# dt from x/rms under a scaled w_dt, the third block of x loaded one step earlier, and a new order of the opening

## The chip, the cores and the metric

The kernel runs on one core of one Trainium2 chip. Its engines work side by side, each through its own queue in order: PE (TensorE, the matmuls; "PEld" in the profile is its loading of weights), DVE (VectorE), ACT (ScalarE), POOL (GpSimd) and SP (SyncE), which here only issues DMAs. The metric is the device time of one execution in microseconds; less is better.

## The reference

One step of a streaming encoder layer for a prompt of 1024 tokens and a sample of 32, width 1024:

```python
shift, scale, gate = split(silu(c) @ w_ada + b_ada, 3)
hn   = rmsnorm(x, norm_g) * (1 + scale) + shift
proj = hn @ w_in       # lru_x | lru_gate | xBC | z | dt_raw, 1024+1024+1536+1024+16 columns
...
dt = softplus(dt_raw + dt_bias)
# RG-LRU on lru_x, chunked SSD scan on xBC with dt, grouped RMSNorm, gates
out = x + gate * (concat[y_lru, y_ssd] @ w_out)
y = rmsnorm(out, final_norm_g)
```

`dt_raw` is the last 16 columns of the projection, one per SSD head. The convolution and scan states are further outputs.

## The kernel before

All activations lie with channels on the 128 partitions and tokens along the free axis. The 1056 tokens are cut into three blocks: 384, 384 and 256 + 32 (the last 32 are the sample, which has its own scale and shift). A projection of 128 output columns is called a unit; for each block it takes 8 channel groups times 3 matmuls, since every fp32 operand is split in a rounded part (`whi`, `hb[..., 0]`) and a rest (`wlo`, `hb[..., 1]`): hi x hi, hi x lo, lo x hi.

The **opening** is what comes before the main loops. It must make `hb` (x/rms times the scale, as hi and lo) for the three blocks out of x and of `w_ada`, and meanwhile it computes the first three units (24, 25, 26) with what is ready. Its order on all engines is written by hand as a list of tokens, `PROG` (lines 46 to 60), under a manual schedule; a loop (lines 373 to 457) turns each token into instructions, and each engine runs its own in that order. The tokens that matter here, with block b and channel group k:

- `q`, `a`, `f`: squares of x on ACT (L179), their sums on DVE (L182, L185). `c`, `r`, `v`, `b`: sum over channels on PE (L192), root, reciprocal, spread over partitions on PE (L211). `x`: x times 1/rms in place, two groups at a time, on DVE (L217).
- `s`, `o`, `k`, `A`: a pair of `w_ada` units on PE (L120, fp32, 32 weight columns, four partition quarters in turn), its row on ACT (L424), columns of it on PE (L127), the scale `Acol` on DVE (L428). Pairs 0, 2, 4, 6 are the scale's, 8, 10, 12, 14 the shift's, whose columns come at once in `K`; `S` makes the shift (L433) and puts it in two extra columns of the third block's `hb`.
- `h`, `l`: `hb` hi on ACT (L224) and lo on DVE (L228) for one group of one block. `H`, `L`: the split of a unit's weight (L405, L409). `m`, `t`: a group's two hi matmuls and its lo matmul for one unit (L355). `p`: a finished bank is parked in SBUF (L363). `z`: dummy matmuls.
- `w`, `W`: `w_dt` split in hi and lo (L438, L440) as 32 weight columns. `d`, `D`: dt of a block out of `hb` hi and lo (L284, 16 matmuls a block; the shift goes through the two extra columns). `e`, `E`: copies of dt to `dtp` (L289). At the end the shift's part is added (L459) and dt is turned to tokens on partitions and its two halves summed by `selD` (L467).

Loads stand in a second list, `LOADS` (line 45), issued by SP in that order: `x00` is block 0 from group 0, `w` a unit's weight, `s` a `w_ada` pair of 1 MB (three buffers: the next one waits until its buffer's pair was used), `d` is `w_dt`. x has two buffers, so block 2 (`x20`, `x24`) can be loaded only when block 0 has been read for the last time: by `l07`.

The work behind the opening is ordered by a scheduler that simulates the program: units 27 and 16, then for each of eight SSD head pairs two units and the pair's small matmuls (transposes xsT, states dS, yd, yo), then the RG-LRU groups and the output projection, whose ACT and DVE orders are partly by hand.

Of the kernel before, what the change touches and what calls it, by code (L numbers as in the profile page):

```python
# [8 lines left out]
F32 = mybir.dt.float32  # L9
F32R = mybir.dt.float32r  # L10
# [3 lines left out]
D = 1024  # L14
# [29 lines left out]
FIRST = (24, 25, 26)  # L44
LOADS = "x00 x02 x04 x06 w s w s w s x10 x14 s d s s s s x20 x24".split()
PROG = (
# [13 lines left out]
).split()  # L60
# [3 lines left out]
def encoder_step(ctx: ExitStack, tc: tile.TileContext, a, o):  # L64
# [203 lines left out]
    wdt = st.tile([128, KT, 16], F32, name="wdt")  # L268
    wd = st.tile([128, KT, 32], F32R, name="wd")
    dtp = st.tile([32, TW], F32, name="dtp")  # L270
    dsb = st.tile([32, 2], F32, name="dsb")
    selD = st.tile([32, 16], F32, name="selD")
    root = st.tile([128, 1], F32, name="root")
# [4 lines left out]

    def dt_half(b, i):
        if i == 0:  # L280
            pds[b] = pbank([32, BLK[b][1]], "pdt")
        for kk in range(4 * i, 4 * i + 4):
            for q in range(2):
                nc.tensor.matmul(pds[b], lhsT=wd[:, kk, :], rhs=hb[b][:, kk, q, :], start=(kk + q == 0),  # L284
                                 stop=(kk + q == KT))

# [19 lines left out]
    with tc.manual_schedule(engines={E.SP, E.PE, E.Activation, E.DVE, E.Pool}):  # L306
# [8 lines left out]
        for i in (64, 96):  # L315
            nc.gpsimd.tensor_add(sel, sel, ident[:, i:i + 32])
        nc.gpsimd.tensor_add(selD, ident[0:32, 0:16], ident[0:32, 16:32])

# [7 lines left out]
        left_loads = list(LOADS)  # L326
        seen = set()


        def load_next():  # L330
            t = left_loads[0]
            if t == "s":
                n = len(sraw)
                if n >= 3 and 2 * n - 6 not in paired:
                    return False
                sraw.append(st.tile([128, 2, KT, 128], F32, name="sraw", tag="sraw", bufs=3))
                u = (2 * n + KT) % (2 * KT)
                last[0] = dma(sraw[n], a["w_ada"][u:u + 2].rearrange("i p k n -> p i k n"))
            elif t == "w":
                ws.append(fetch_unit(a["w_in"][FIRST[len(ws)]]))  # L340
            elif t == "d":
                dma(wdt, a["w_dt"])
            else:
                if t == "x20" and "l07" not in seen:
                    return False
                last[0] = load_x(int(t[1]), int(t[2]))
            left_loads.pop(0)
            return True

        last, paired = [None], set()  # L350

# [21 lines left out]
        for t in PROG:  # L373
            while left_loads and load_next():
                pass
            c = t[0]
            n = [int(q) for q in t[1:]] if c in "qxhlmtdac" else int(t[1:] or 0)
            if c == "z":
# [58 lines left out]
            elif c == "w":  # L437
                nc.scalar.copy(wd[:, :, 0:16], wdt)  # L438
            elif c == "W":
                nc.vector.tensor_sub(wd[:, :, 16:32], wdt, wd[:, :, 0:16].bitcast(F32))  # L440
            elif c == "d":
                dt_half(*n)
            elif c == "e":
                dt_out(n)
            elif c == "D":
                dt_half(2, 0)
                dt_half(2, 1)
            elif c == "E":
                dt_out(2)
                nc.vector.tensor_copy(dsb, pds[2][:, 288:290])  # L450
            elif c == "y":
# [13 lines left out]
    for c in range(9):  # L465
        t0, L = (c * 128, 128) if c < 8 else (S0, TS)
        nc.tensor.matmul(pt[0:L, c, :], lhsT=dtp[:, t0:t0 + L], rhs=selD, start=True, stop=True)  # L467
    for (L, c0, n) in ((128, 0, 8), (32, 8, 1)):
# [644 lines left out]
```

## Time and profile before

| | us |
|---|---|
| runs: median (lowest to highest of 3) | 776.29 (775.0 to 776.35) |
| the profiled execution | 775.32 |
| its span in the profile | 773.6 |

The profile takes one execution; 1.7 us of its time lie outside the span. A row of the time line reads: start, length, engine, line of the kernel, operation, output<-inputs, and in brackets the engine's idle time before it with what ended that. A row of the table by stretches reads: the stretch, its length, then busy time and count of PE, PEld, DVE, ACT and POOL (or of PE alone), the clock granted to PE as a share of the full one, the busy share of the DMA engines, and GB/s.

### The profile page before, as it was taken

The page shows a single profiled execution, that of the slowest core. Times are in us where ns is not written, and L with a number is a line of the kernel's source. Part 1 is how long each engine was busy: PE and PEld are TensorE (multiplying, and loading weights), DVE is VectorE, ACT ScalarE, POOL GpSimd, SP SyncE. Part 2 cuts the span into 40 slices and gives each one's busy share as a digit, 9 for nine tenths or more (in the row PEclk, how much of TensorE's full clock was granted, in tenths as well). Part 3 has the DMA queues.
Part 4 walks back from the last instruction along what each step waited for, and adds up shares of the span by engine and source line. Part 5 has one row for each costly group of instructions (what it writes and reads, how often), then busy time and mean ns, then how long its engine had stood idle before and what let it go on. Part 6 is the DMA issues. An engine that isn't in the chain of part 4 may idle for free.

```text
span 773.6 us, 12733 instructions
## 1 busy us (share of the span) xinstructions
PE 756.6 (98%) x5100; PEld 730.2 (94%) x5100; DVE 533.2 (69%) x861; ACT 413.3 (53%) x599; POOL 46.7 (6%) x159
## 2 busy tenths in 40 slices
PE   8989999999999999999999999999999999999994
PEld 8868999999999999999999999999999999999994
DVE  5754877888878777788376557546668897535643
ACT  5544764334426344253676977696777664323430
POOL 1000310001000000000011001100101000000000
PEclk9999999999999999999999999999999999999998
DMA  9750124443343434333222112011144685654841
GB/s 331 305 198 28 58 59 122 133 161 112 123 134 100 149 111 122 111 99 124 80 62 65 61 35 62 28 54 42 44 140 136 192 281 164 221 147 137 261 118 69
DMA packets 40059, 96.31 MB, mean 124 GB/s; under 512 B 4408, under 2 KB 22080, under 8 KB 40000
## 3 DMA queue, kind: packets, MB, share of 16 engines
q1 hardware_dynamic: 40000, 95.49, 38.8%
q8 instruction: 40, 0.66, 0.3%
q14 instruction: 19, 0.16, 0.1%
HBM read 85.53 MB, written 9.95 MB: 123 GB/s over the span
## 4 chain that ended last, share of the span: by engine, by line
PE 85%; DVE 6%; DMA 5%; ACT 2%; issue 1%; SPq 1%; POOL 0%; POOLq 0%; DVEq 0%; ACTq 0%
PE pj L236 16%; PE pj L238 16%; PE pj L237 16%; PE mix L943 6%; PE mix L941 6%; PE mix L942 6%; PE pj L355 3%; PE yd L688 2%; PE dS L663 2%; DMA sraw<-in_w_ada_dram 2%; PE yo L703 2%; PE ada_s L120 1%; PE xsT L647 1%; PE gt L825 1%; PE gt L827 1%; PE gt L826 1%
## 5 line engine op out<-in xcount | busy, mean ns | idle before, releaser
L236 PE MATMUL pj<-hb,whi 128*128 128x384 f32 (+1 forms) x792 | 260.1, 328 | 0.0
L237 PE MATMUL pj<-hb,whi 128*128 128x384 f32 (+1 forms) x792 | 259.5, 328 | 0.0
L238 PE MATMUL pj<-hb,wlo 128*128 128x384 f32 (+1 forms) x792 | 259.4, 327 | 0.0
L101 ACT CAST whi<-wraw 128x1024 fp32r<-128x1024 f32 x81 | 84.9, 1048 | 138.1 <-PE mix L942 68.4
L238 PEld LDWEIGHTS pj<-hb,wlo 128*128 128x128 f32 x792 | 150.0, 189 | 1.6 <-issue 1.5
L236 PEld LDWEIGHTS pj<-hb,whi 128*128 128x128 f32 x792 | 149.4, 189 | 1.9 <-issue 1.7
L237 PEld LDWEIGHTS pj<-hb,whi 128*128 128x128 f32 x792 | 150.0, 189 | 1.2 <-issue 1.1
L103 DVE TENSOR_TENSOR wlo<-wraw,whi 128x1024 fp32r<-128x1024 f32 x81 | 98.6, 1219 | 48.0 <-ACT whi L101 48.0
L943 PE MATMUL mix<-yt,wlo 128*128 128x324 f32 (+2 forms) x320 | 103.9, 326 | 0.4 <-DVE wlo L103 0.4
L941 PE MATMUL mix<-yt,whi 128*128 128x324 f32 (+2 forms) x320 | 104.1, 325 | 0.0
L942 PE MATMUL mix<-yt,whi 128*128 128x324 f32 (+2 forms) x320 | 103.7, 324 | 0.0
L498 DVE SCALAR_TENSOR_TENSOR u<-raw,par,u 128x1060 f32<-128x1060 f32 x60 | 78.5, 1311 | 1.5 <-ACT u L496 1.1
L943 PEld LDWEIGHTS mix<-yt,wlo 128*128 128x128 f32 x320 | 60.0, 188 | 0.8 <-DVE wlo L103 0.7
L941 PEld LDWEIGHTS mix<-yt,whi 128*128 128x128 f32 x320 | 60.1, 188 | 0.2
L942 PEld LDWEIGHTS mix<-yt,whi 128*128 128x128 f32 x320 | 60.0, 188 | 0.1
L255 ACT ACTIVATE raw<-pj,sb 128x256 f32<-128x256 f32 (+1 forms) x74 | 30.9, 468 | 25.4 <-PE pj L238 14.6
L631 DVE TENSOR_TENSOR_SCAN M<-M,mask 128x1060 f32<-128x1060 f32 x16 | 37.8, 2363 | 9.1 <-DMA M<-dA_d 9.1
L355 PE MATMUL pj<-hb,whi 128*128 128x384 f32 (+1 forms) x144 | 38.5, 339 | 2.5 <-ACT hb L224 2.5
L960 DVE SCALAR_TENSOR_TENSOR ot<-mix,gate,xr 128x352 f32<-128x352 f32 (+3 forms) x32 | 14.8, 489 | 26.2 <-PE mix L943 21.2
L355 PEld LDWEIGHTS pj<-hb,whi 128*128 128x128 f32 x144 | 25.1, 189 | 7.0 <-ACT hb L224 3.5
L634 ACT ACTIVATE M<-M 128x1060 f32<-128x1060 f32 x16 | 17.5, 1092 | 25.9 <-DVE M L631 24.0
L299 POOL COPY cso<-raw 128x3 f32<-128x3 f32 x20 | 15.8, 789 | 230.6 <-ACT raw L255 230.6
(231 smaller groups left out, 1098.7 us busy)
## 6 DMA issues: line engine op xcount, KB each, us to landing
wraw<-in_w_out_dram SPq DMA_DIRECT2D x48, 512.0 KB, 3.7
wraw<-in_w_in_dram SPq DMA_DIRECT2D x36, 512.0 KB, 3.7
M<-dA_d SPq DMA_DIRECT2D x16, 530.0 KB, 4.5
sraw<-in_w_ada_dram SPq DMA_DIRECT2D x8, 1024.0 KB, 11.2
E<-E_d SPq DMA_DIRECT2D x16, 265.0 KB, 4.4
yz_d<-y SPq DMA_DIRECT2D x8, 530.0 KB, 4.2
wraw<-in_w_ada_dram SPq DMA_DIRECT2D x8, 512.0 KB, 5.0
x<-in_xh_dram SPq DMA_DIRECT2D x4, 384.0 KB, 4.8
```

Source lines behind the costliest of these rows:

```text
L101: nc.scalar.copy(hi, raw)
L103: eng.tensor_sub(lo, raw, hi.bitcast(F32))
L236: nc.tensor.matmul(out, lhsT=hi[:, kk, :], rhs=hh, start=(kk == 0), stop=False)
L237: nc.tensor.matmul(out, lhsT=hi[:, kk, :], rhs=hl, start=False, stop=False)
L238: nc.tensor.matmul(out, lhsT=lo[:, kk, :], rhs=hh, start=False, stop=(kk == KT - 1))
L255: nc.scalar.activation(dst[0:P, off + d:off + d + e - s], banks[b][0:P, s:e], func, bias=sb[0:P, w:w + 1])
L355: nc.tensor.matmul(banks[u][b], lhsT=w[i][:, k, :], rhs=hb[b][:, k, 0 if heads else 1, :], start=(heads and k == 0 and i == 0), stop=(not ...
L498: nc.vector.scalar_tensor_tensor(u, raw[:, k:k + TW], wcol(k), u, op0=OP.mult, op1=OP.add)
L631: nc.vector.tensor_tensor_scan(M, M, mask, 0.0, op0=OP.add, op1=OP.mult)
L941: nc.tensor.matmul(ps, lhsT=w[0][:, k, :], rhs=yh, start=(half == 1 and k == 0), stop=False)
L942: nc.tensor.matmul(ps, lhsT=w[0][:, k, :], rhs=yl, start=False, stop=False)
L943: nc.tensor.matmul(ps, lhsT=w[1][:, k, :], rhs=yh, start=False, stop=(half == 0 and k == KT - 1))
```

## The change

It has three parts.

1. dt is no longer computed from `hb` but from x/rms itself: w_dt is multiplied by the scale (`wda`, one for the prompt, one for the sample), padded from 16 to 32 columns with zeros, and the eight channel groups go in fp32 into four partition quarters of one bank, two groups each. The shift's part is its own small product (`P`, `Q`) of `shift` with the unscaled, padded `wdp`. `dtp` has 128 rows now, and the transposing matmul sums the four quarters by `sel`. The copies of dt to `dtp` have 128 partitions instead of 32, the same columns.
2. In `LOADS` x's third block stands ahead of the last `w_ada` pair. It may be loaded when `l07` and `d0` are through, since `d0` now reads the first block's x.
3. `PROG` is a new order of all these tokens.

```diff
-LOADS = "x00 x02 x04 x06 w s w s w s x10 x14 s d s s s s x20 x24".split()
+LOADS = "x00 x02 x04 x06 w s w s w s x10 x14 s d s s s x20 x24 s".split()
 PROG = (
-        "z34 q00 q02 a02 q04 a04 q06 H0 a06 f0 L0 c0 s0 r0 v0 b0 o0 H1 k0 x00 A0 L1 h00 z6 s2 A1 l00 h01 m000 "
...
+    "z34 q00 q02 a02 q04 a04 q06 a06 H0 f0 L0 c0 r0 s0 v0 H1 b0 o0 L1 z1 k0 A0 A1 z1 s2 x00 x02 h00 o2 z1 "
...
-    wd = st.tile([128, KT, 32], F32R, name="wd")
-    dtp = st.tile([32, TW], F32, name="dtp")
-    dsb = st.tile([32, 2], F32, name="dsb")
-    selD = st.tile([32, 16], F32, name="selD")
+    wdp = st.tile([128, KT, 32], F32, name="wdp")
+    wda = st.tile([128, 2, KT, 32], F32, name="wda")
+    dtp = st.tile([128, TW], F32, name="dtp")
+    dsb = st.tile([128, 2], F32, name="dsb")
...
-    def dt_half(b, i):
-        if i == 0:
-            pds[b] = pbank([32, BLK[b][1]], "pdt")
-        for kk in range(4 * i, 4 * i + 4):
-            for q in range(2):
-                nc.tensor.matmul(pds[b], lhsT=wd[:, kk, :], rhs=hb[b][:, kk, q, :], start=(kk + q == 0),
-                                 stop=(kk + q == KT))
+    def dt_block(b):
+        pds[b] = pbank([128, XB[b][1]], "pdt")
+        for (s, e, w) in h_parts(b):
+            for kk in range(KT):
+                q = slice(32 * (kk % 4), 32 * (kk % 4) + 32)
+                nc.tensor.matmul(pds[b][q, s:e], lhsT=wda[:, w, kk, :], rhs=xin[b][:, kk, s:e], start=(kk < 4),
+                                 stop=(kk >= 4))
+
+    def dt_shift():
+        ps = pbank([128, 2], "pds")
+        for kk in range(KT):
+            q = slice(32 * (kk % 4), 32 * (kk % 4) + 32)
+            nc.tensor.matmul(ps[q, :], lhsT=wdp[:, kk, :], rhs=shift[:, kk, :], start=(kk < 4), stop=(kk >= 4))
+        return ps
...
-        nc.gpsimd.tensor_add(selD, ident[0:32, 0:16], ident[0:32, 16:32])
+        nc.gpsimd.memset(wdp, 0.0)
+        nc.gpsimd.memset(wda, 0.0)
...
-                if t == "x20" and "l07" not in seen:
+                if t == "x20" and not {"l07", "d0"} <= seen:
...
             elif c == "w":
-                nc.scalar.copy(wd[:, :, 0:16], wdt)
-            elif c == "W":
-                nc.vector.tensor_sub(wd[:, :, 16:32], wdt, wd[:, :, 0:16].bitcast(F32))
+                nc.gpsimd.tensor_copy(wdp[:, :, 0:16], wdt)
+                for w in range(2):
+                    nc.vector.tensor_mul(wda[:, w, :, 0:16], wdt, Acol[:, :, w:w + 1].to_broadcast([128, KT, 16]))
...
-        nc.tensor.matmul(pt[0:L, c, :], lhsT=dtp[:, t0:t0 + L], rhs=selD, start=True, stop=True)
+        nc.tensor.matmul(pt[0:L, c, :], lhsT=dtp[:, t0:t0 + L], rhs=sel[:, 0:16], start=True, stop=True)
```

What the new order does on ACT around the squares of x's third block (x_420). Before, with the second block's hb tiles as hb_84 and the third's as hb_85:

```order
L424 COPY hrow<-ada_s 128x256
L179 ACTIVATE xacc<-x_420 128x2x288
L179 ACTIVATE xsq<-x_420 128x2x288 x3
L224 ACTIVATE hb_84<-x_140,Acol 128x384 x4
L202 ACTIVATE xrs<-xbc,eps 128x2
L202 ACTIVATE xrs<-xbc,eps 32x1
L224 ACTIVATE hb_85<-x_420,Acol 128x256
```

The same place in the changed kernel:

```order
L224 ACTIVATE hb_84<-x_141,Acol 128x384 x3
L431 COPY hrow<-ada_s 128x256
L224 ACTIVATE hb_84<-x_141,Acol 128x384
L179 ACTIVATE xacc<-x_420 128x2x288
L179 ACTIVATE xsq<-x_420 128x2x288 x3
L224 ACTIVATE hb_84<-x_141,Acol 128x384
L431 COPY hrow<-ada_s 128x256
```

Four hb tiles of the second block stood behind the squares; one does now.

PE's dt matmuls stood together before: all of the shift's columns, then two blocks, and the third block's after its first unit:

```order
L355 MATMUL pj_461<-hb_84,whi 128x384
L127 MATMUL ada_c<-sel,hrow 128x2 x8
L284 MATMUL pdt<-hb_84,wd 32x384 x16
L284 MATMUL pdt<-hb_83,wd 32x384 x16
L355 MATMUL pj_669<-hb_85,whi 128x290
```

Now the first block's stands behind its last projection (first piece's place in the program), ahead of a `w_ada` pair:

```order
L211 MATMUL xbc<-ident,xrs 128x128 x3
L362 MATMUL pj_123<-hb_83,whi 128x384
L284 MATMUL pdt<-x_124,wda 32x384 x8
L120 MATMUL ada_s<-sraw,sc 32x256 x8
L362 MATMUL pj_445<-hb_84,whi 128x384
```

The first block's dt has moved from the end of the second block to the end of the first, with half as many matmuls, of fp32; the third block's stands within the second block's projections, and the second's at their end.

On DVE behind the opening, in the second head pair's loop: the convolution u of the next pair (three steps, L498) before, among the scans of M (L631) and the work on y:

```order
L498 SCALAR_TENSOR_TENSOR u<-raw,par,u 128x1060
L631 SCALAR_TENSOR_TENSOR M<-M,mask 128x1060
L707 TENSOR_TENSOR y<-y,yo 128x512
L248 COPY sb<-pj_1756 128x2
L635 TENSOR_TENSOR M<-M,CBm 128x1060
L707 TENSOR_TENSOR y<-y,yo 128x32
L498 SCALAR_TENSOR_TENSOR u<-raw,par,u 128x1060
L635 TENSOR_TENSOR M<-M,CBm 128x1060
L747 TENSOR_SCALAR gate<-ada_c,par 128x2
L498 SCALAR_TENSOR_TENSOR u<-raw,par,u 128x1060
```

and in the changed kernel (L503 is the same line, L636 the scan):

```order
L503 SCALAR_TENSOR_TENSOR u<-raw,par,u 128x1060
L677 SCALAR_TENSOR_TENSOR dS<-dS,dec_bc 128x64
L696 SCALAR_TENSOR_TENSOR y<-u,par,yd 128x512
L677 SCALAR_TENSOR_TENSOR dS<-dS,dec_bc 128x64
L503 SCALAR_TENSOR_TENSOR u<-raw,par,u 128x1060
L696 SCALAR_TENSOR_TENSOR y<-u,par,yd 128x32
L677 SCALAR_TENSOR_TENSOR dS<-dS,dec_bc 128x64 x2
L711 TENSOR_TENSOR yo<-yo,E 128x384
L248 COPY sb<-pj_1748 128x2
L503 SCALAR_TENSOR_TENSOR u<-raw,par,u 128x1060
L636 SCALAR_TENSOR_TENSOR M<-M,mask 128x1060
```

The convolution's three steps stand ahead of both scans now. On PE the transposes that read this u stand 49 projection matmuls earlier than before, at the 422nd behind the opening instead of the 471st.

More of the change, by code (lines that the diff above doesn't have):

```diff
@@ L326, in encoder_step @@
         left_loads = list(LOADS)
-        seen = set()
+        seen, last, paired = set(), [None], set()
         def load_next():
@@ L348, in load_next @@
             return True
-        last, paired = [None], set()
         def mm(u, b, k, heads):
@@ L376, in encoder_step @@
             c = t[0]
-            n = [int(q) for q in t[1:]] if c in "qxhlmtdac" else int(t[1:] or 0)
+            n = [int(q) for q in t[1:]] if c in "qxhlmtac" else int(t[1:] or 0)
             if c == "z":
@@ L437, in encoder_step @@
             elif c == "w":
-                nc.scalar.copy(wd[:, :, 0:16], wdt)
-            elif c == "W":
-                nc.vector.tensor_sub(wd[:, :, 16:32], wdt, wd[:, :, 0:16].bitcast(F32))
+                nc.gpsimd.tensor_copy(wdp[:, :, 0:16], wdt)
+                for w in range(2):
+                    nc.vector.tensor_mul(wda[:, w, :, 0:16], wdt, Acol[:, :, w:w + 1].to_broadcast([128, KT, 16]))
             elif c == "d":
-                dt_half(*n)
+                dt_block(n)
             elif c == "e":
                 dt_out(n)
[L445 to L450, printed above, removed]
+            elif c == "P":
+                aps["d"] = dt_shift()
+            elif c == "Q":
+                nc.vector.tensor_copy(dsb, aps["d"])
             elif c == "y":
```

24 rows, old and new, of the table PROG are left out of this document.

## The prediction

> **What bounds the kernel now.** I read the page first, then the chain that ended last, then the busy time of TensorE (PE) by stretches.
>
> ```profile
> PE 756.6 (98%) x5100; PEld 730.2 (94%) x5100; DVE 533.2 (69%) x861; ACT 413.3 (53%) x599; POOL 46.7 (6%) x159
> PE 85%; DVE 6%; DMA 5%; ACT 2%; issue 1%; SPq 1%; POOL 0%; POOLq 0%; DVEq 0%; ACTq 0%
> ...
> 38.00:52.00 14.00, 11.35 (x73) 9.61 (x72) 7.23 (x13) 7.00 (x15) 0.00 (x0) 1.00 0.75 273
> 200.00:400.00 200.00, 199.51 (x1452) 191.96 (x1451) 152.41 (x258) 90.58 (x121) 8.52 (x53) 1.00 0.36 113
> 400.00:600.00 200.00, 200.00 (x1237) 199.34 (x1236) 126.39 (x144) 154.07 (x214) 18.34 (x38) 1.00 0.23 68
> ```
>
> PE is the bound, and past the opening it hardly stops (199.51 of 200 us, then 200 of 200). So the time can fall in two ways only: PE gets less to do, or it waits less in the opening, the first 79.5 us, where the chain's DMA, DVE and ACT shares lie. Everything behind is then shifted as one piece, if its own chains on DVE and DMA come early too.
>
> Where does PE wait in the opening? In three places.
>
> ```profile
> 17.95 20.22 SPq L338 DMA_DIRECT2D sraw<-in_w_ada_dram  x4
> 38.26 0.97 SPq L171 DMA_DIRECT2D x<-in_xh_dram  x2
> ...
> 43.73 0.34 PE L355 MATMUL pj<-hb,whi 128*128 128x384 f32 x1
> 44.43 0.69 ACT L179 ACTIVATE xacc<-x 128x576 f32<-128x576 f32 x1 [3.83 <-DMA x<-in_xh_dram]
> 45.14 0.33 PE L355 MATMUL pj<-hb,wlo 128*128 128x384 f32 x1
> 45.93 1.27 ACT L179 ACTIVATE xsq<-x 128x576 f32<-128x576 f32 x2 [0.24 <-DMA x<-in_xh_dram]
> 47.10 2.12 ACT L224 ACTIVATE hb<-x,Acol 128x384 fp32r<-128x384 f32 x4
> 47.76 0.44 PE L355 MATMUL pj<-hb,whi 128*128 128x384 f32 x1 [2.28 <-ACT hb L224]
> ...
> 50.87 0.67 PEld L192 LDWEIGHTS xbc<-ones,xacc 128*128 128x128 f32 x6 [0.66 <-issue]
> ```
>
> ACT stands still for 3.83 us until the third block of x lands at 44.4, squares it, and only then makes the second block's hb tiles 4 to 7; PE wants tile 4 from 45.3 on and gets it at 47.76. The eight matmuls from 43.73 to 45.14 start 0.176 us apart, so the pause is 2.62 - 0.18 = **2.4 us**. The sum over the third block (L192) comes behind the same squares: 0.66 idle less a pitch, **0.5 us**.
>
> ```profile
> 69.01 0.19 PEld L355 LDWEIGHTS pj<-hb,whi 128*128 128x128 f32 x1 [0.49 <-ACT hb L224]
> 69.48 0.33 PEld L355 LDWEIGHTS pj<-hb,whi 128*128 128x128 f32 x2 [0.18 <-DVE hb L228]
> 70.09 0.33 PEld L355 LDWEIGHTS pj<-hb,whi 128*128 128x128 f32 x2 [0.17 <-DVE hb L228]
> 70.70 0.19 PEld L355 LDWEIGHTS pj<-hb,whi 128*128 128x128 f32 x1 [0.18 <-DVE hb L228]
> ```
>
> In the third block PE overtakes the hb tiles once more: 0.49 + 0.18 + 0.17 + 0.18 = **1.0 us**.
>
> **The change part by part.** *dt.* These rows carry it: the old dt matmuls, the shape nearest to the new ones, and a row of tiny ones.
>
> ```profile
> 59.26 1.84 PE L127 MATMUL ada_c<-sel,hrow 128*128 128x2 f32 x16
> 60.96 5.76 PE L284 MATMUL pdt<-hb,wd 128*32 128x384 f32 x32
> 70.94 2.29 PE L284 MATMUL pdt<-hb,wd 128*32 128x290 f32 x16
> 28.23 1.07 PE L120 MATMUL ada_s<-sraw,sc 128*32 128x256 f32 x16
> 28.91 0.28 DVE L440 TENSOR_TENSOR wd<-wdt,wd 128x128 fp32r<-128x128 f32 x1
> ```
>
> The old ones take PE from 60.96 to about 66.55 and from 70.94 to 73.07: 5.6 + 2.1 = 7.7 us with nothing beside them. The new ones have L120's pattern, plain fp32 with 32 weight columns, four partition quarters in turn (eight matmuls are sixteen records). L120 takes 1.07 us at 256 columns. At 384 columns I take 1.07 x 1.5, less its drain, 1.5 us, twice; 1.07 for the third block's 256 columns; and for its 32 columns and the shift's 2, where only L127's sixteen records in 1.84 us are near and have four times the weight columns, 0.45 each. Sum 5.0, so **-2.7 us**. Bounds: 3.2 us if columns cost nothing more and the small pieces nothing, 6.4 if the wide ones take 1.6 each and the small ones L120's 1.07: -4.5 to -1.3. Weights under the scale are two DVE products of L440's size (0.28 each) instead of one; they stand at about 33 us, between PE's first block's last tiles, for which DVE is some 0.8 us ahead. Were that cover gone, 0.3 us. ACT loses one cast. POOL (6% busy) clears two tiles and copies w_dt; behind that copy stand only the borders of the three parked tiles, which convolutions want some 40 us later.
>
> *The start.* The new order puts the second weight's rounding ahead of the first ada row on ACT.
>
> ```profile
> 14.01 0.37 ACT L424 COPY srow<-ada_s 128x256 f32<-128x256 f32 x1 [1.44 <-PE ada_s L120]
> 14.28 1.05 ACT L405 CAST whi<-wraw 128x1024 fp32r<-128x1024 f32 x1
> 15.86 1.22 DVE L409 TENSOR_TENSOR wlo<-wraw,whi 128x1024 fp32r<-128x1024 f32 x1
> 15.98 0.62 ACT L224 ACTIVATE hb<-x,Acol 128x384 fp32r<-128x384 f32 x1 [0.65 <-DVE Acol L428]
> 21.43 1.07 PE L120 MATMUL ada_s<-sraw,sc 128*32 128x256 f32 x16 [0.98 <-DMA sraw<-in_w_ada_dram]
> ```
>
> The cast starts with its weight's landing (about 14.05), ends at 15.1, the row copy at 15.5; on DVE the rest (1.22) now stands before Acol and x: 15.1 to 16.4, Acol to 16.75, x's first pair (0.95) to 17.7, and hb tile 0 comes at 18.4 instead of 16.6. PE's first projection starts at 18.45 instead of 17.62. But the third ada pair waits for its landing in both (21.43), and the fourth for its own (28.23). What remains is work not done by then: by the order 40 of the first block's 72 matmuls stand before the fourth pair, now 35. Five at 0.176: **+0.9 us**, paid later.
>
> *The third block of x.* Its DMA now waits for d0, which reads the first block's buffer, and stands ahead of the last ada pair. From 28.23 PE has: L120 and its switch 1.1, 37 matmuls 6.5, ada columns, sum and spread about 1.8, d0 1.5, so d0 ends near 39.1, 0.8 us after the old issue at 38.26. The transfer is then alone in the queue.
>
> ```profile
> wraw<-in_w_in_dram SPq DMA_DIRECT2D x36, 512.0 KB, 3.7
> x<-in_xh_dram SPq DMA_DIRECT2D x2, 576.0 KB, 6.2
> ```
>
> Against 6.2 us behind an ada pair I take 3.8 for it (the row of 512 KB): 43.0, its second half 44.5, the last pair near 47.1. On ACT hb tiles 0 to 6 of block two now stand before the squares, and tile 7 behind them is wanted only after 126 of the 144 matmuls of both blocks: the 2.4 us go. On PE the second block's first 42 matmuls (7.4) and three ada pairs (3.3) follow d0, so L192 comes at 49.8; DVE has its sum at about 48.9 (six tails and x's four products to 45.5, three additions 2.3, the last tail 0.6, the halves 0.45). That cover is 0.9 us: the 0.5 goes. Next: shift's columns end near 54.0, the shift itself 54.9, dt_shift at 55.7; x's last pair 56.0, where d2 starts at 56.2. Then 21 matmuls (3.7) and d1 give the third block a start near 62.9, with hb tiles ready by 61.1: the 1.0 goes.
>
> Sum: -2.7 - 2.4 - 0.5 - 1.0 + 0.9 = **-5.7 us** against the profiled execution's 775.32, so 769.6. The runs' median, 776.29, lies 0.97 above that execution; I forecast from the median: **770.6 us**.
>
> *Behind the opening* PE's order differs only by when small matmuls are slipped in, up to the fifth SSD head pair; I cost that at nothing, between -0.5 (what the row from 200 to 400 us loses) and the price of the first rival.
>
> **The rivals.**
>
> (a) The new order asks too early. By the order the third xsT stands 49 projection matmuls earlier.
>
> ```profile
> 173.48 1.32 DVE L498 SCALAR_TENSOR_TENSOR u<-raw,par,u 128x1060 f32<-128x1060 f32 x1
> 182.78 1.09 ACT L751 ACTIVATE u<-u 128x1060 f32<-128x1060 f32 x1 [0.73 <-DVE u L498]
> 185.53 1.15 PE L647 MATMUL xsT<-ident,u 128*128 128x128 f32 x9
> ```
>
> Its u was ready at 183.87, 1.7 us ahead. 49 x 0.162 (two wide pitches and one of 0.135) is 7.9 us; if DVE keeps its old pace PE waits 6.2 us and the result is 776.8, no change. Against it: DVE's order has moved the same convolution ahead of two scans of 2.4 us. For it: that planner's durations are not these rows. 12% for 3 us or more.
>
> (b) The third block lands as late as now, 6.2 us after its issue: 45.3, so L192 waits 2.4 - 0.9 = 1.5 us: 772.1. Its queue is empty then, which speaks against it. 10%.
>
> (c) The clock falls near the start.
>
> ```profile
> 46.25:49.66 3.41, 1.90 (x9) 1.00 0.82 333
> 80.38:83.80 3.42, 3.42 (x29) 1.00 0.49 153
> 83.80:87.21 3.41, 3.41 (x15) 0.50 0.60 178
> ```
>
> After a stretch of 3.41 us with the tiny dt transposes the granted clock is 0.50 for one such stretch, a loss of 1.7; 1.90 busy of 3.41 was enough to keep it. At 15.0 to 18.4 the new start has about 1.8 busy (an ada pair 1.07, its columns 0.4, two dummies), with three dummies in all where six stood. One stretch costs at most 1.7: 772.3. 8%. The same 1.7 may go in the other direction, if the stretches fall otherwise over the transposes.
>
> The Trainium skill, "TensorE: Matmul & The Clock Gate", section "What's actually happening", says the PE clock halves after at least one idle window of about 3.4 us. By that rule the new start, never idle so long, loses nothing; the row at 83.80 shows a loss without an idle window, so I keep the chance.
>
> (d) Slower. The four quarters of the new dt matmuls run one after another. L120's sixteen records take 1.07 us as four groups of four, 0.27 a group; one after another they would take 0.27 each, 4.3 us, and at 384 columns 6.4. Then d0 and d1 cost 6.4 each, d2 4.3, the small pieces as before 0.9: 18.0 instead of 5.0, and the result is 783.6. From 10.7 us in all (more than twice my value) the change loses. L120 speaks against it: it has the same four quarters. 3%.
>
> **How the numbers follow.** Forecast 67%, (a) 12%, (b) 10%, (c) 8%, (d) 3%. Low end: -4.5 for dt instead of -2.7, and a clock stretch less: 767.0. High end: dt at -1.3 and (b), or half of (a): 774.6. What this kernel's measurement can tell from no change is about 0.2%, 1.6 us. Forecast, (b), (c) and the half of (a) that costs 3 us are faster: 91%; the other half no change: 6%; slower (d): 3%.
>
> **What would show it.** Right: no ACT wait for x before block two's hb tiles; no PE gap of 2 us at 45; L284 at 384 columns near 1.5 us; the opening's last projection near 73.5 to 74 instead of 79.5; and the SSD stage without new PE waits. Wrong: L284 well over 2 us, PE waiting for L192's halves near 50, a second row of clock 0.50, or PE waiting for u, dS or M between 100 and 250 us.

## The result and the profile after

| | before | after |
|---|---|---|
| median, us | 776.29 | 767.31 |
| lowest | 774.65 | 765.56 |
| the profiled execution | 775.32 | 765.56 |
| its span | 773.6 | 763.8 |
| opening: start of the first matmul behind its last projection | 79.55 | 72.25 |

The ratio of the times is 0.9882, with a 95% interval from 0.9864 to 0.9900: 9.0 us faster, where 5.7 were forecast. One of the changed kernel's five runs took 814.3 us at a mean granted clock of 0.85; it counts in the median but not in the ratio. A second set of runs of both kernels (e0_after below) gave 0.9881 (0.9858 to 0.9905).

The page of the changed kernel, its busy times and the shares of the chain that ended last:

```profile
PE 748.8 (98%) x5126; PEld 724.4 (95%) x5126; DVE 533.6 (70%) x862; ACT 417.9 (55%) x602; POOL 48.0 (6%) x161
PE 88%; DMA 6%; DVE 4%; ACT 1%; issue 1%; SPq 1%; DVEq 0%; ACTq 0%
```

PE is busy 7.8 us less, and its share of the chain rises from 85% to 88% at the cost of DVE (6 to 4) and ACT (2 to 1): the waits of the opening went. TensorE in the opening, time line of the changed kernel:

```profile
37.60 1.50 PE L284 MATMUL pdt<-x,wda 128*32 128x384 f32 x16
38.91 1.05 PE L120 MATMUL ada_s<-sraw,sc 128*32 128x256 f32 x16
...
49.80 0.62 PE L192 MATMUL xbc<-ones,xacc 128*128 128x1 f32 x5
...
52.25 1.95 PE L127 MATMUL ada_c<-sel,hrow 128*128 128x2 f32 x16
...
55.82 0.31 PE L291 MATMUL pds<-shift,wdp 128*32 128x2 f32 x16
55.97 1.18 PE L284 MATMUL pdt<-x,wda 128*32 128x256 f32 x32
57.07 0.97 PE L362 MATMUL pj<-hb,whi 128*128 128x384 f32 x4
...
60.97 1.50 PE L284 MATMUL pdt<-x,wda 128*32 128x384 f32 x16
62.40 0.40 PE L362 MATMUL pj<-hb,whi 128*128 128x290 f32 x1
...
72.25 2.02 PE L472 MATMUL dtT<-sel,dtp 128*128 128x16 f32 x18
```

No row has an idle time in brackets. The length in a row runs to a modelled end; what a piece costs is the distance from its start to the next start: d0 38.91 - 37.60 = 1.31, dt_shift 0.15, d2 1.10, d1 1.43. The same in the table by stretches, from the fourth ada pair to the end of the opening (first row before, second after):

```profile
28.23:79.55 51.32, 48.42 (x349) 40.32 (x349) 30.25 (x62) 24.08 (x56) 2.30 (x3) 1.00 0.36 133
```

```profile
28.09:72.25 44.16, 44.16 (x386) 37.82 (x387) 28.41 (x62) 24.64 (x56) 4.64 (x14) 1.00 0.43 156
```

51.32 us become 44.16, and PE is busy in all of them. Split by the line of each matmul record, each counted up to the next start:

| from the fourth ada pair on, us | before | after | measured change | forecast |
|---|---|---|---|---|
| its start | 28.23 | 28.09 | -0.14 | 0 |
| dt (L284, L291) | 7.73 | 4.00 | -3.73 | -2.7 |
| three pauses within the projections: 2.44, 0.52 and 1.12 | 4.08 | none | -4.08 | -3.9 |
| five projection matmuls more at 0.176 | | | +0.88 | +0.9 |
| switches between kinds, the small pieces | | | -0.23 | 0 |
| sum: the opening's end | 79.55 | 72.25 | -7.30 | -5.7 |

Soon behind the opening the two traces are 9.0 us apart; they are 9.1 to 9.2 apart from 220 us to 600 and 9.7 at the last matmul. The first 1.7 us behind the opening are the clock. Two rows of the changed kernel:

```profile
70.54:73.96 3.42, 3.42 (x30) 3.42 (x28) 3.42 (x6) 2.89 (x6) 1.62 (x2) 1.00 0.39 109
73.96:77.37 3.41, 3.41 (x27) 3.35 (x27) 3.41 (x4) 0.43 (x3) 2.99 (x6) 1.00 0.57 163
```

The dt transposes run from 72.25 to 74.19, so 1.71 of their 1.94 us are in the first row. The stretch behind it has clock 1.00, where the kernel before had 0.50. In the output projection the old trace has a wait of TensorE (0.37 us idle at 616.92) that the new one lacks, and the traces move 0.59 apart there. That is not shown to come from the change: the second trace of the changed kernel (e0_after) has such a wait again, 0.18 us. From 200 to 400 us:

```profile
200.00:400.00 200.00, 198.95 (x1452) 190.77 (x1451) 147.19 (x251) 94.13 (x129) 7.97 (x53) 1.00 0.35 108
```

PE loses 1.05 us in this stretch, where it lost 0.49 before.

### The profile page after: what moved, and what is told of

Same layout as the page of the kernel before. It is cut to its first block, busy times and chain, and to the rows that moved or that the text cites. A ratio compares the mean times of both kernels' runs of the same rounds, so it can differ in the third digit from the quotient of the medians.

```text
span 763.8 us, 12803 instructions
## 1 busy us (share of the span) xinstructions
PE 748.8 (98%) x5126; PEld 724.4 (95%) x5126; DVE 533.6 (70%) x862; ACT 417.9 (55%) x602; POOL 48.0 (6%) x161
## 4 chain that ended last, share of the span: by engine, by line
PE 88%; DMA 6%; DVE 4%; ACT 1%; issue 1%; SPq 1%; DVEq 0%; ACTq 0%
PE pj L236 15%; PE pj L238 15%; PE pj L237 15%; PE mix L948 8%; PE mix L946 8%; PE mix L947 8%; PE pj L362 4%; PE yd L693 2%; PE dS L668 2%; DMA sraw<-in_w_ada_dram 2%; PE yo L708 1%; DMA wraw<-in_w_in_dram 1%; PE ada_s L120 1%; DMA M<-dA_d 1%; PE xsT L652 1%; PE gt L830 1%
## 5 line engine op out<-in xcount | busy, mean ns | idle before, releaser
L237 PEld LDWEIGHTS pj<-hb,whi 128*128 128x128 f32 x792 | 149.3, 189 | 1.1 <-issue 0.9
L236 PEld LDWEIGHTS pj<-hb,whi 128*128 128x128 f32 x792 | 148.8, 188 | 1.4 <-issue 1.3
L503 DVE SCALAR_TENSOR_TENSOR u<-raw,par,u 128x1060 f32<-128x1060 f32 x60 | 78.6, 1312 | 1.5 <-ACT u L501 1.1
L636 DVE TENSOR_TENSOR_SCAN M<-M,mask 128x1060 f32<-128x1060 f32 x16 | 37.7, 2361 | 10.7 <-DMA M<-dA_d 10.7
L842 DVE SCALAR_TENSOR_TENSOR r<-a,r 128x1060 f32<-128x1060 f32 x8 | 10.1, 1263 | 28.2 <-ACT r L841 28.2
L813 ACT CAST uh<-u 128x1060 fp32r<-128x1060 f32 x8 | 8.6, 1077 | 37.3 <-DVE u L503 37.3
```

What stands on the lines that cost most here:

```text
L236: nc.tensor.matmul(out, lhsT=hi[:, kk, :], rhs=hh, start=(kk == 0), stop=False)
L237: nc.tensor.matmul(out, lhsT=hi[:, kk, :], rhs=hl, start=False, stop=False)
L503: nc.vector.scalar_tensor_tensor(u, raw[:, k:k + TW], wcol(k), u, op0=OP.mult, op1=OP.add)
L636: nc.vector.tensor_tensor_scan(M, M, mask, 0.0, op0=OP.add, op1=OP.mult)
```

## The experiments

Each was timed beside the kernel before on the same chip. Medians of the kernel before were 776.28 beside e0_after, e1_order, e1_order_load and e2_olddt, 774.72 beside e3_load, e3_order2, e4_start and e5_spread, and 774.21 beside the other four, so ratios are compared rather than times.

**e0_after.** The changed kernel, unedited.

> The changed kernel once more, for its spread and for the clock. In the two traces at hand 1.7 us of the difference is one 3.41-us stretch at clock 0.50 over the dt transposes, there before the change and not after it. Theory: whether the stretch comes is a matter of where the 3.41-us stretches happen to begin in an execution, in both kernels alike; then the times of each kernel fall into two groups some 1.7 us apart (765.6 and 767.4 here; 774.9 and 776.5 before), and the medians differ by about 7.3 + 0.5 us when both draw alike. Rival: the change itself removed it; then the old kernel always has it, the new one never, and the new kernel's times lie within 0.5 us of each other near 765.6.

Measured: 766.73 us (765.48 to 769.27), ratio 0.9881. Neither holds as stated: the six times spread over 3.8 us, and not in two groups. The time that an execution loses to the clock, (1 - mean clock) times the time, can be estimated for each. It is 6.2 us on average over the 29 executions of the kernel before on this chip and 5.1 over these six, so some 1 us of the difference is the clock's, an estimate with an uncertainty about as large as itself. With the loss taken off, the medians are 770.1 and 762.0 us, 8.1 apart: 7.3 of it is the opening's, and the rest is not assigned. The third and the fourth ada pair started 0.6 us later than in the first trace, with their landings; that moved the opening's end from 72.25 to 72.84.

**e1_order.** The kernel before; in `PROG`, hb tiles 4 to 7 of the second block ahead of the squares:

```diff
...
-m110 m111 q20 l13 t102 t110 q22
+m110 m111 h14 h15 h16 h17 q20 l13 t102 t110 q22
...
```

> The kernel before, with only block two's hb tiles 4 to 7 moved ahead of the squares of x's third block on ScalarE. Theory (the 2.4-us pause of TensorE is this order and nothing else): the pause at 45 goes, the sum over the third block is then reached 2.4 us earlier and waits for DVE about 1 us, so 1.5 to 2.4 us off the time before, about 774.3. Rival (the wait is only passed on to the sum over the third block, which needs the same late landing): the sum waits 2 us or more and the time falls by less than 0.7.

Measured: 776.98 us, ratio 1.0006 (0.9987 to 1.0026). The theory fell. The rival has the time right, but not the place: the sum over the third block waits 0.5 us as before. TensorE and VectorE of this kernel:

```profile
50.69 0.79 PE L355 MATMUL pj<-hb,whi 128*128 128x384 f32 x3 [2.75 <-DVE hb L228]
```

```profile
48.49 1.62 DVE L182 TENSOR_TENSOR xacc<-xacc,xsq 128x576 f32<-128x576 f32 x2 [0.32 <-ACT xsq L179]
50.03 2.20 DVE L228 SCALAR_TENSOR_TENSOR hb<-x,Acol,hb 128x384 fp32r<-128x384 f32 x4
```

The pause is no shorter, 2.9 us by the starts of its matmuls. The hi tiles are early now, but their tails stand on DVE behind the additions of the same late squares.

**e1_order_load.** The same, and the load order of the change:

```diff
-LOADS = "x00 x02 x04 x06 w s w s w s x10 x14 s d s s s s x20 x24".split()
+LOADS = "x00 x02 x04 x06 w s w s w s x10 x14 s d s s s x20 x24 s".split()
```

> The same, and the third block of x loaded ahead of the shift's last pair, as in the change, with the old dt. Theory: it lands about 1.5 us earlier, the sum over the third block no longer waits, and 2.9 us of the time before are gone, about 773.4. Rival (the earlier landing buys nothing beyond the order): within 0.4 us of the kernel with the order alone.

Measured: 774.11 us, ratio 0.9972 (0.9953 to 0.9990), about 2.2 us faster. The stretch from the fourth ada pair to the opening's end is 49.36 us instead of 51.32. So the load does what the order alone didn't. Not all of the theory came: x landed at 37.79 us instead of 44.41, but pauses of 0.7 us before the tails and 0.5 us at the sum are left.

**e3_load.** The load order alone (the diff above on the kernel before).

> The kernel before, with only the load order changed: x's third block ahead of the shift's last pair, every engine's order as before. Reason: in the old order the last pair waits for its buffer (issue at 37.8) and x behind it in the same queue; put ahead it is issued near 33 and lands near 38 and 39, before ScalarE comes to its squares (40.6). Theory (the late landing alone made TensorE's two pauses of 2.4 and 0.5 us): both go without any other edit, the stretch from the fourth ada pair to the last projection of the opening falls from 51.3 to about 48.4 us, and the median from 776.3 to about 773.4. Rival (the order on ScalarE or VectorE is needed as well): a pause of over 1 us stays, and the stretch is over 49.4.

Measured: 772.77 us, ratio 0.9972 (0.9955 to 0.9989), 2 us faster; the stretch is 47.98 us, 3.3 shorter. ScalarE, which waited 3.83 us for x at this place before:

```profile
42.10 0.37 ACT L424 COPY hrow<-ada_s 128x256 f32<-128x256 f32 x1 [0.38 <-PE ada_s L120]
42.37 0.69 ACT L179 ACTIVATE xacc<-x 128x576 f32<-128x576 f32 x1
42.95 1.25 ACT L179 ACTIVATE xsq<-x 128x576 f32<-128x576 f32 x2
44.46 0.69 ACT L179 ACTIVATE xsq<-x 128x576 f32<-128x576 f32 x1 [0.25 <-DVE xacc L182]
45.05 2.12 ACT L224 ACTIVATE hb<-x,Acol 128x384 fp32r<-128x384 f32 x4
```

The squares don't wait, the tiles behind them are in time, and both pauses of TensorE are gone without any change of an engine's order. The theory holds for the opening. ScalarE's new order on top of the load (e1_order_load) even made this stretch 1.4 us longer. Not all of it arrived: by 166 us the profiled execution had given back 2.7 us, the most of it in two waits of TensorE for dS (1.1 and 0.9) behind scans on DVE. DVE waited for M's DMA for 9.7 us between 80 and 260 us instead of 4.9; the changed kernel waits 7.7 us for it without such a loss.

**e3_order2.** The kernel before; the order alone, but on ACT and DVE:

```diff
...
-m110 m111 q20 l13 t102 t110 q22
+m110 m111 h14 h15 h16 h17 l14 l15 l16 l17 q20 l13 t102 t110 q22
...
```

> The kernel before with the old load order, and block two's hb tiles 4 to 7 with their tails moved ahead of the squares of x's third block on ScalarE and of the squares' additions on VectorE (the order alone on ScalarE left a pause of 3.1 us before the first tail). Theory: the tiles' pause goes whole, the sum over the third block still waits about 1 us for the late landing; the stretch from the fourth ada pair to the opening's last projection is about 49.4 us (51.3 before), the median about 774.4. Rival (the pause is passed on to the sum): the sum waits over 2 us and the stretch stays within 0.7 of 51.3.

Measured: 774.80 us, ratio 0.9997 (0.9980 to 1.0014). TensorE of this kernel:

```profile
47.74 0.34 PE L355 MATMUL pj<-hb,wlo 128*128 128x384 f32 x1
49.80 0.73 PE L192 MATMUL xbc<-ones,xacc 128*128 128x1 f32 x6 [1.72 <-DVE xacc L185]
```

```profile
47.23:50.64 3.41, 1.70 (x12) 1.37 (x11) 1.87 (x3) 0.51 (x2) 0.00 (x0) 1.00 0.62 252
50.64:54.05 3.41, 3.41 (x12) 3.12 (x13) 0.60 (x3) 0.32 (x2) 0.00 (x0) 0.50 0.02 5
```

The tiles' pause is gone, and the sum over the third block takes its place. The times are the rival's: no gain. The trace lies between the two. The sum waits 1.9 us by the starts, a little less than the rival's 2. The stretch is 51.44 us, but 51.32 less the two old pauses (2.44 and 0.52) and with the new one (1.9) is only 50.2, between the theory's 49.4 and the rival's 50.6; the 1.2 us above it are the clock's, by this estimate.

**e2_olddt.** The changed kernel with the old dt, in the changed kernel's places:

```diff
...
-t071 b1 p01 t072 d0 x10 p02
+t071 b1 p01 t072 d00 d01 x10 p02
...
-                nc.tensor.matmul(pds[b][q, s:e], lhsT=wda[:, w, kk, :], rhs=xin[b][:, kk, s:e], start=(kk < 4),
-                                 stop=(kk >= 4))
+                nc.tensor.matmul(pds[b], lhsT=wd[:, kk, :], rhs=hb[b][:, kk, q, :], start=(kk + q == 0),
+                                 stop=(kk + q == KT))
```

> The changed kernel with the old dt (fp32r weights in two parts on the finished hb tiles, at the places of the new d0 and d1, and after the third block's first weight for block three). Theory from the account of the trace after (7.73 us of dt before, 4.00 after): 3.7 us slower than the changed kernel, about 771.0 against 767.3. Rival (the prediction's own size of the term): 2.7 us, about 770.0. If dt were not what gained, within 1 us.

Measured: 772.35 us, ratio 0.9958 (0.9941 to 0.9976) against 0.9881: some 6 us slower than the changed kernel. In the opening dt takes 7.83 us instead of 4.00, and the stretch from the fourth pair 47.59 instead of 44.16, 3.4 us more, near the theory's 3.7. The total fits neither the theory nor the rival. The other 2.6 us come behind the opening: the two traces are 3.8 us apart until 140 us and 6.4 from 350 us on. One thing more differs here: dt no longer reads x, so x's third block is issued at 34.98 us and lands at 38.85, 4.2 us earlier than in the changed kernel.

**e9_d2late.** The order of the SSD stage was suspected: with old dt it is the old one, in the changed kernel a new one.

```diff
...
-m151 x26 m152 P h23 l20 d2 h24 Q l21 h25 l22 t150 t151 e2 t152
+m151 x26 m152 h23 l20 h24 l21 h25 l22 t150 t151 t152
...
-m270 t270 y0 m201
+m270 t270 y0 d2 e2 P Q m201
...
```

> The changed kernel with the third block's dt matmuls and dt_shift put where the old ones stood, behind the first weight of block three; nothing else is edited, but with dt finished at that place all engines' order of the SSD stage falls back almost to that of before (the order of TensorE there differs from before in 82 lines instead of 1150). Theory (the old SSD order asks too early once the opening is shorter, and only the order made anew carries the gain through; the kernel with old dt lost 2.6 us that way between 110 and 350 us, its trace against the changed kernel's, and the one with the load order alone 2.7): the opening's length as the changed kernel's within 0.3 us, new TensorE waits of 1 to 2.7 us in the SSD stage, and a median 1 to 2.5 us above the changed kernel's 766.7 to 767.3. Rival (the SSD order is worth nothing): within 0.5 us of it.

Measured: 767.35 us, ratio 0.9899 (0.9868 to 0.9929). The opening keeps its length (44.17 us), and in the SSD stage the trace loses 0.25 us against the changed kernel's; from 200 to 400 us PE is busy 199.50 us. The theory fell: the SSD order is worth nothing that these runs can tell.

**e4_start.** The changed kernel with more work ahead of the third and fourth ada pair:

```diff
...
-t001 A3 s4 h02 L2 h03 m011 l01
+t001 A3 h02 m011 m020 s4 L2 h03 l01
...
-m012 l03 m020 h04
+m012 l03 h04
...
-t031 s6 x06 t032 a16 m040 o6
+t031 t032 m040 s6 x06 a16 o6
...
```

> The changed kernel with two matmul units of the first block put ahead of the third ada pair and two ahead of the fourth, where TensorE waited for w_ada (0.69 and 0.48 us in the trace after, 1.76 and 0.49 in the second one). Theory (the start's cost is work that isn't done by those landings): 0.7 and 0.5 us, less where a landing comes early; the opening's last projection 1.0 us earlier, the median 0.5 to 1.2 below the changed kernel's 766.7 to 767.3. Rival (the wait comes back at the next thing that hangs on the same ada columns): within 0.3 us.

Measured: 767.12 us (764.56 to 768.50), ratio 0.9897 (0.9872 to 0.9922). From the fourth pair on the opening takes 43.66 us instead of 44.16, so the 0.5 is there in the trace; but the pairs landed later in this execution and the times don't tell the kernels apart:

```profile
21.88 1.07 PE L120 MATMUL ada_s<-sraw,sc 128*32 128x256 f32 x16 [0.37 <-DMA sraw<-in_w_ada_dram]
28.68 0.64 PE L120 MATMUL ada_s<-sraw,sc 128*32 128x256 f32 x8 [0.29 <-DMA sraw<-in_w_ada_dram]
```

**e5_spread.** The changed kernel; the additions to `dtp` behind `e1` (token `B`), and a transpose (`T`) behind each of nine projection units:

```diff
...
-t240 m250 t250 m260 t260 m270
+t240 T0 m250 t250 T1 m260 t260 T2 m270
...
```

> The changed kernel with its nine tiny dt transposes spread between the third block's projections instead of one after another in 2.0 us. Theory (a 3.41-us stretch at clock 0.50 comes when too much of the stretch ahead of it goes to such matmuls, by the luck of where stretches begin): it can't come there any more; the fastest times change by less than 0.5 us (nine switches between projections against nine in a row), but the upper part of the spread (up to 1.7 us above) thins out, the median 0.3 to 1.0 below the changed kernel's. Rival (stretches come elsewhere, or have another cause): median and spread as the changed kernel's, 766.7 to 767.3, or up to 1 us slower by the switches.

Measured: 765.99 us (765.69 to 768.86), ratio 0.9895 (0.9869 to 0.9921). The switches cost nothing that shows (the trace is 0.4 us behind the changed kernel's, with landings 0.5 later), but executions up to 3 us above the lowest remain. The median is in the theory's range, the ratio to the kernel before is the rival's: inconclusive.

**e8_dtT2.** The changed kernel, the dt transposes issued twice:

```diff
-    for c in range(9):
+    for c in (0, 1, 2, 3, 4, 5, 6, 7, 8) * 2:
```

> The changed kernel with its nine dt transposes issued twice, the same results written over, so that some 4 us of tiny matmuls stand in a row, longer than one stretch of 3.41 us. Theory (a stretch at clock 0.50 follows a stretch in which too much of TensorE's time goes to tiny matmuls): it now follows in the profiled execution and in nearly all runs: 2.0 us for the matmuls and 0.8 to 1.7 more than the changed kernel's share of such stretches, together about 770. Rival (the transposes have no part in it): no row of clock 0.50 within 7 us behind them, and 2.0 us slower, about 769. The SSD order moves with the edit, so the clock's rows decide, the time only beside them.

Measured: 768.62 us (768.42 to 769.64). The stretches of 3.41 us under and behind the transposes (73.74 to 77.74), and then the two rows where the clock did fall:

```profile
72.57:75.98 3.41, 3.41 (x31) 3.35 (x30) 3.41 (x5) 2.91 (x4) 1.58 (x3) 1.00 0.41 118
75.98:79.40 3.42, 3.42 (x29) 3.37 (x30) 3.42 (x4) 0.69 (x1) 2.95 (x6) 1.00 0.27 80
52.09:55.51 3.42, 3.42 (x26) 3.38 (x26) 3.11 (x8) 2.39 (x8) 0.00 (x0) 1.00 0.00 0
55.51:58.92 3.41, 3.41 (x52) 1.98 (x52) 3.11 (x13) 1.90 (x8) 0.00 (x0) 0.50 0.00 0
```

2.24 us of transposes in one stretch did not bring the clock down, so the theory falls for the new dt. The fall came elsewhere, behind the shift's sixteen tiny column matmuls (52.22 to 54.03).

**e7_pairs.** The changed kernel; dt's quarters in pairs:

```diff
-                q = slice(32 * (kk % 4), 32 * (kk % 4) + 32)
+                q = slice(32 * (kk // 2), 32 * (kk // 2) + 32)
```

> The changed kernel with dt's four partition quarters taken in pairs (0 0 1 1 2 2 3 3) instead of in turn (0 1 2 3 0 1 2 3); the sums are the same. In the trace after, four starts stand 0.007 us apart and the next four 0.32 us later, the time of one 384-column pass. Theory (matmuls of different quarters run beside each other, of the same quarter one behind the other, and the issue is in order): a pair's second matmul waits for the first and holds the other quarters back, so d0 and d1 take between 1.6 and 5.1 us each instead of 1.31 and 1.43, and the time rises by 0.6 to 9 us. Rival (the order of the quarters doesn't matter): d0 and d1 as before, the time within 0.5 us of the changed kernel's.

Measured: 767.63 us, ratio 0.9898 (0.9856 to 0.9940). TensorE of this kernel:

```profile
38.45 1.52 PE L284 MATMUL pdt<-x,wda 128*32 128x384 f32 x16
39.76 1.07 PE L120 MATMUL ada_s<-sraw,sc 128*32 128x256 f32 x16
```

1.31 us, as before: the rival holds, the order of the quarters doesn't matter. Whether one quarter for all eight matmuls would cost more was not tried.

**e6_best.** The changed kernel with the edits of e4_start (one unit more, `m021`, ahead of the third pair) and e5_spread, and

```diff
-LOADS = "x00 x02 x04 x06 w s w s w s x10 x14 s d s s s x20 x24 s".split()
+LOADS = "x00 x02 x04 x06 w s w s w s x10 s x14 d s s s x20 x24 s".split()
```

> The changed kernel with three edits at once: three matmul units ahead of the third ada pair and two ahead of the fourth; the fourth pair's w_ada loaded ahead of the second half of x's second block; the dt transposes spread between projections. Theory (of the start only the landing of the third pair, near 21.2 to 21.9, is left to wait for; the fourth then lands near 26): TensorE waits under 0.4 us at the third pair and not at the fourth, the opening's last projection stands 1.2 us earlier than the changed kernel's 72.3 to 72.8 less the transposes now inside it, and the median is 1 to 2 us below 766.7 to 767.3. Rival (the later half of x's second block takes the place of the wait, at the sum over the second block near 33): no gain, or up to 1 us slower.

Measured: 766.36 us (765.23 to 766.59), ratio 0.9882 (0.9853 to 0.9911). At both pairs no wait over 0.2 us is left, but one comes up where the rival has it, at the sum over the second block:

```profile
31.53 0.34 PE L363 MATMUL pj<-hb,wlo 128*128 128x384 f32 x1
32.38 0.83 PE L193 MATMUL xbc<-ones,xacc 128*128 128x1 f32 x6 [0.51 <-DVE xacc L186]
```

The last matmul stands 0.5 us earlier than the changed kernel's. The six times lie within 1.4 us, but by its ratio it is no faster: these runs don't show that it beats the changed kernel.

## Why the prediction was right, and where it was not

**The direction, and the walk.** The bound was PE with three pauses in the opening, and the change gave it less to do and took the pauses. The DMAs of x's third block in the changed kernel, SP's queue in the time line and the issues between 30 and 50 us (the last number is the median time to landing):

```profile
39.16 0.92 SPq L171 DMA_DIRECT2D x<-in_xh_dram  x2
```

```profile
x<-in_xh_dram SPq DMA_DIRECT2D x2, 576.0 KB, 4.5
```

The walk came out: issue at 39.16 (forecast 39.1), landing at 43.1 and 44.7 by the trace (43.0 and 44.5), the sum over it at 49.80 (49.8), the shift's columns done at 54.06 (54.0), dt_shift at 55.82 (55.7). Rival (b), a landing 6.2 us after the issue, is out: it took 3.9 and 5.1.

**The term that was mis-sized: dt, -2.7 forecast, -3.73 measured.** The wide pieces cost 1.31 and 1.43 (1.5 each was taken). A row's length, 1.07 for L120, runs to the modelled end, and only part of its drain was taken off: its four groups start 0.215 apart, and 4 x 0.215 x 1.5 is 1.29. The two small pieces were taken at 0.45 each from L127's sixteen records; dt_shift costs 0.15 and the 32 columns about 0.24 (1.10 less four groups at 0.215). The nearest row had four times the weight columns, and it misled. Rival (d), quarters one after another, is out: d0 would have taken 6.4.

**The sum and the walk ended in different places.** By the walk the third block's projections began at 62.9; with its 72 matmuls at 0.135 that ends at 72.6. The terms gave 73.5 to 74, and the two were not compared. Measured: 62.40 and 72.25. That the walk came so near is in part luck: from 28.23 to 72.6 it has 44.4 us, of which 5.0 are dt and 39.4 all else, where the trace has 4.00 and 40.16, so an error of +1.0 and one of -0.8 cancel.

**The range.** 767.31 lies just above its low end, 767.0, which was built from a dt 1.8 us cheaper and one clock stretch less; the trace has 1.0 of the first and the whole of the second. The high end, 774.6, does not come out of its terms: dt at -1.3 with (b) makes 773.5, and half of (a) 773.7.

**The pauses: the sizes were right, the cause is shown in part.** 2.4, 0.5 and 1.0 us went as forecast (4.08 by the records). The prediction had the 2.4 us go because hb tiles 0 to 6 now stand ahead of the squares on ACT. In the changed kernel they do, and DVE's tails stand ahead of the additions as well; ACT and DVE there:

```profile
42.55 0.62 ACT L224 ACTIVATE hb<-x,Acol 128x384 fp32r<-128x384 f32 x1
43.12 0.69 ACT L179 ACTIVATE xacc<-x 128x576 f32<-128x576 f32 x1
46.07 0.60 ACT L224 ACTIVATE hb<-x,Acol 128x384 fp32r<-128x384 f32 x1
```

```profile
42.58 2.20 DVE L228 SCALAR_TENSOR_TENSOR hb<-x,Acol,hb 128x384 fp32r<-128x384 f32 x4
44.70 2.47 DVE L182 TENSOR_TENSOR xacc<-xacc,xsq 128x576 f32<-128x576 f32 x3
```

In the old kernel the same moves gain nothing. e1_order moved tiles 4 to 7 on ACT, and the pause stayed, with DVE's tails in place of ACT's tiles; e3_order2 moved both, and the sum over the third block waited instead. e3_load moved one DMA and both pauses went. In the old order x's third block stood in SP's queue behind the shift's last pair, which waited for a buffer until 37.80, and it landed at 44.41. In the changed kernel its issue waits for d0 and is even later than before (39.16 instead of 38.26); it lands at 43.1, only 1.3 us earlier, since its first half takes 3.9 us instead of 6.2. PE's order helped there, too: with d0 and a third ada pair ahead of it, PE comes to tile 4 at 48.74 us, where the old one wanted it from 45.3 on. How much of the load, of the order on ACT and DVE and of PE's order is needed was not tried apart in the changed kernel.

**The start: +0.9 forecast, +0.88 measured.** e4_start took 0.5 of it back in its trace. Both pairs follow the landings of their w_ada, which vary by some 0.6 us between executions of one kernel.

**Behind the opening: costed at nothing, -0.1 in the trace's SSD stage.** Rival (a) is out: xsT waits 1.1 us in all instead of 0.5. e9_d2late shows that the new SSD order isn't needed for the gain either. What stays open is why e2_olddt and e3_load gave back 2.6 and 2.7 us between 110 and 350 us with a shorter opening, and e1_order_load and e9_d2late only 0.2 and 0.25; late M transfers go with it in e3_load, but the changed kernel has nearly as much of them, and the order does not explain it.

**The clock: kept out of the sum, and in the profile it is the largest piece of the error.** One stretch at 0.50 fell over the old transposes and none over the new, 1.7 us, named in the prediction as a possibility beside rival (c). The first trace does not show that the new transposes are spared it, since a boundary cut them there (see the last section). Over many executions it is worth some 1 us, by the estimate under e0_after. Rival (c) itself, a fall near the start, was in neither trace of the changed kernel, though in the traces of e1_order and e3_load, which have the old start. Nor is 1.90 us busy of 3.41 safe, as the prediction took it: in e1_order 1.88 us were followed by a fall and 1.61 us, later, were not.

The sum of the profiled executions: -7.30 for the opening, -1.72 for the clock, -0.13 for the SSD stage, -0.59 in the output projection (most of which e0_after does not have), -9.74 at the last matmul; 775.32 - 765.56 is 9.76.

## What to carry to other kernels

A wait that shows on one engine's order may be made by a DMA's place in its queue: move the load alone before reordering the engines behind it. What a piece of work costs an engine in line is the distance from its start to the next start, not the length in its row. When a sum of terms and a walk through the time line give different ends, find out why before giving a number.

## What the runs showed of the hardware that was not expected

Before the end of the program, the granted clock falls to 0.50 for one stretch of 3.41 us in 7 of the 14 traces, at four places: behind the dt transposes (before, e1_order_load), in the wait for the third ada pair (e1_order, e3_load), in the wait for the third block's sum (e3_order2), and behind the shift's column matmuls (e7_pairs, e8_dtT2). First the old dt transposes (the group of line 467 in the kernel before, whose last column is rows x weight columns and the shapes), then the wait for the third ada pair in e3_load:

```profile
L467 PE MATMUL dtT<-selD,dtp x18: 178/258/279, 80.7 to 82.7; 32*128 32x16 f32 x16, 32*32 32x16 f32 x2
```

```profile
18.59:22.00 3.41, 1.74 (x16) 1.45 (x18) 3.41 (x7) 1.55 (x4) 0.00 (x0) 1.00 1.03 379
22.00:25.42 3.42, 3.42 (x21) 2.28 (x22) 1.11 (x2) 1.51 (x3) 0.00 (x0) 0.50 1.05 392
```

The old transposes use 32 of the 128 rows; where all of them lay in one stretch (before, e1_order_load) the clock fell behind it, where a boundary cut them (e1_order, e2_olddt, e3_load, e3_order2) it did not. The new ones use 128 rows, and 2.24 us of them in one stretch were not enough (e8_dtT2). Nor were all nine, 1.95 us, in one stretch of e7_pairs (74.68 to 76.63):

```profile
73.34:76.75 3.41, 3.41 (x31) 3.35 (x30) 3.41 (x5) 2.92 (x4) 1.39 (x2) 1.00 0.32 88
76.75:80.17 3.42, 3.42 (x26) 3.42 (x27) 3.42 (x5) 0.52 (x1) 3.35 (x6) 1.00 0.56 161
```

Rows alone don't decide it: the shift's column matmuls use 128 rows and 2 columns, and where all sixteen lay in one stretch the clock fell behind them in two traces (e7_pairs, e8_dtT2, 1.81 us of them) and not in two others (e1_order, e3_load, 1.70 us). All this would fit a clock that follows how much of the array works and not only whether it idles, but the runs don't show that: stretches with 1.6 to 1.9 us busy (e9_d2late, e1_order, e0_after) were not followed by a fall, and others with 1.7 to 1.9 were.

The Trainium skill, "TensorE: Matmul & The Clock Gate", section "What's actually happening", asks for an idle window of about 3.4 us before the clock halves. The Trainium skill calls the window free-running in the same section, and so it looks here: where the transposes fall in a stretch differs from trace to trace. The length agrees with these stretches of 3.41 too; the condition doesn't: in none of the seven was PE idle for a whole stretch, and in four it was busy throughout.

Eight fp32 matmuls with 32 weight columns into four partition quarters took 1.31 us for 384 columns, whether the quarters came in turn or in pairs (e7_pairs), and 0.98 for 256 in turn, from their start to the next start.
